# Conditioning weights from the SP queue to GpSimd's queue, with three buffers of their own

## The chip, the cores and the metric

The kernel runs on one core of a Trainium2 chip, as one program. The metric is the device time of one execution in microseconds. The kernel before took 1189.63, 1191.67 and 1193.36 us in three runs, median 1191.67. One more execution was recorded by the hardware profiler; the rows of the profile below are of that one.

## The reference, cut to what matters

Two layers of a decoder trunk work on 256 tokens of width 1024. Each layer has three sub-layers: a SwiGLU feed-forward, a token mixer (gated linear recurrence in layer 0, chunked gMLP in layer 1) and a second feed-forward. Every sub-layer is wrapped by two norms and by a shift, a scale and a gate, which come from one vector `c`:

```
cond = silu(c)
mod  = (cond @ ada_w[i] + ada_b[i]).reshape(9, 1024)      # 3 sub-layers x (shift, scale, gate)

def sublayer(x, fn, pre_g, post_g, shift, scale, gate, res_w):
    h = rms_norm(x, pre_g) * (1.0 + scale) + shift
    return x + res_w * gate * rms_norm(fn(h), post_g)
```

The matrix `ada_w` of the two layers has 2 x 1024 x 9216 float32 values. The kernel holds it as 144 tiles of 128 x 1024, that is 144 x 512 KB. These are the conditioning weights. The other weights are those of the feed-forwards and the mixers.

## The kernel before

**Stages.** The six sub-layers run one behind the other: ffn0, the recurrence (hg), ffn1, ffn2, the gMLP (gm) and ffn3. Each takes the normed activations (`h`, transposed, as a high and a low part), multiplies them with blocks of weights on TensorE, and ends in a tail (`tail`, L250): the last output products, the post norm, the new `x`, the next sub-layer's pre norm, and TensorE transposes to the new `h`.

**Weights.** A block of 1 MB comes in two halves (`wblock`, L112). Each half is loaded into one of four `raw` buffers on SP's queue (`load`, L55), ScalarE writes its rounded high part (L119), and VectorE writes the rest as the low part by a subtraction (L120). High and low part stand in tiles `w` of a pool of 12, enough for six blocks. Each product on TensorE is three matmuls: high x high, high x low, low x high. In ffn0 a 128 x 256 product takes three matmuls (`mm3f`, L332); later feed-forwards use `chunk2` (L322), 16 matmuls for a chunk; an output block (`out_mm`, L274) is 24 matmuls of 128 x 512.

**Conditioning.** For each of the 144 tiles, `ada` (L159) loads 512 KB and lets VectorE take the dot product with `cond` (L169: one instruction for the product and its sum, one that reads the sum out); the result is one column of `mod`. The text calls this pair a dot. The buffers are two tiles of the pool `adap`; in the start phase (`ring` is 1) two of three tiles come from the pool `p4` of four buffers instead. `pace` (L134) spreads the tiles over the blocks of weights: `wblock` counts a credit up and calls `ada` when it is due. Some 16 tiles have to be there before ffn0 can start, two for each 128 rows of the first product.

**The gate.** `gate_tile` (L188) turns eight columns of `mod` into the gate tile `G`, 128 x 1024. VectorE scales them (L193), TensorE transposes them (`gps`, L195), ScalarE copies the result (`grow`, L197), and two DMAs on GpSimd's queue write it to DRAM (`gflat`, L199) and read it back, spread to all partitions (`G`, L201). `G` is used in the tail by L259 and L263. Before the change these twelve DMAs are all that is on GpSimd's queue.

**The start.** `start` (L879) loads `c`, `x` in two halves and a few constants, computes `cond` through TensorE (`cps`, L897), the pre norm of `x` (L905 to L917) and transposes it (`xps`, L921). For each 128 rows, `first_h` (L938) then makes shift and `A` from two dots (L944, L945), ScalarE applies them (`hf`, L948) and writes the high part of `h` (L950), and VectorE writes the low part (L951). ffn0's first product (L418) is sorted so that in each of the first seven steps 16 matmuls of high x high stand first, then 16 with the low part of `h`, then 16 with the low part of `w`.

**What sets the order.** The program is written with a tile framework. Its scheduler orders the instructions of each engine by priorities and by a simulated time of its own; tile pools give the buffers, and an instruction that needs a buffer waits until the last reader of the old tile is done. `keep_in_program_order` holds the loads of one queue in the order in which the code issues them. Each engine and each queue takes its instructions strictly in the order that results.

Of the kernel before, what the change touches and what calls it, by code (L numbers as in the profile page):

```python
# [10 lines left out]
F32 = mybir.dt.float32  # L11
# [7 lines left out]
P = 128  # L19
# [14 lines left out]
class Body:  # L34
    def __init__(self, ctx, tc, ins, out):
        self.ctx, self.tc, self.nc, self.out = ctx, tc, tc.nc, out
        self.d = dict(zip(_INS, ins))
        pool = lambda name, bufs, **k: ctx.enter_context(tc.tile_pool(name=name, bufs=bufs, **k))
        self.const = pool("const", 1)
        self.raw = pool("raw", 4)  # L40
        self.whl = pool("whl", 12)
        self.act = pool("act", 1)
        self.adap = pool("adap", 2)
        self.cols = pool("cols", 2)
        self.tiny = pool("tiny", 4)
        self.bcp = pool("bcp", 2)
        self.p4 = pool("p4", 4)
        self.p2 = pool("p2", 4)
        self.scr = pool("scr", 1)
        self.acc = pool("acc", 4, space=PSUM)  # L50
        self.yps = pool("yps", 1, space=PSUM)
        self.dram = pool("dram", 2, space=bass.MemoryType.DRAM)
# [106 lines left out]
    def ada(self, upto):  # L159
        nc = self.nc  # L160
        while self.ada_next < min(upto, 144):
            i = self.ada_next
            if self.ring and i % 3:
                t = self.p4.tile([P, D], F32, tag="t4", name="ada")
            else:
                t = self.adap.tile([P, D], F32, tag="ada", name="ada")
            self.load(t, self.d["ada"][i])
            junk = self.scr.tile([P, D], BF16, tag="junkv", name="junkv")
            nc.vector.tensor_tensor_reduce(junk, t, self.cond, 1.0, 0.0, ALU.mult, ALU.add,  # L169
                                           self.mod[i // 24][:, i % 24:i % 24 + 1])  # L170
            self.ada_next += 1
# [313 lines left out]
    def hgrn(self, hT, G_fn, pre_next, nxt, bg):  # L485
        nc, tc = self.nc, self.tc
# [36 lines left out]

        def gate_f(hb, pr, z):

            L = self.adap.tile([P, 512], F32, tag="ada", name="L")
            c = slice(512 * pr, 512 * pr + 512)
            k, nk, b = kn[hb][:, c], kn[hb][:, H4:][:, c], bq[hb][:, c]
            nc.scalar.activation(L, z, AF.Abs)
            self.act_exp(L, L, scale=-1.0)  # L530
            self.tact(L, L, AF.Ln, bias=1.0)
            nc.vector.scalar_tensor_tensor(b, z, 0.0, L, op0=ALU.min, op1=ALU.subtract)
            nc.vector.scalar_tensor_tensor(nk, z, 0.0, L, op0=ALU.max, op1=ALU.add)
            hs = [(4 * hb + 2 * pr + i, slice(i * S, (i + 1) * S)) for i in range(2)]
            col = lambda a, h: a[:, h:h + 1]
            for h, sl in hs:
                nc.scalar.activation(L[:, sl], b[:, sl], AF.Abs, bias=col(self.ldiff, h))
            for h, sl in hs:
                nc.scalar.activation(b[:, sl], b[:, sl], AF.Relu, bias=col(self.ldiff, h))
            self.act_exp(L, L, scale=-1.0)  # L540
            self.tact(L, L, AF.Ln, bias=1.0)
            for h, sl in hs:
                nc.vector.scalar_tensor_tensor(b[:, sl], b[:, sl], col(self.loglb, h), L[:, sl],
                                               op0=ALU.add, op1=ALU.add)
                nc.vector.tensor_tensor_scan(b[:, sl], self.rmask, b[:, sl], 0.0, ALU.mult, ALU.add)
            for h, sl in hs:
                self.act_exp(k[:, sl], nk[:, sl], scale=-1.0, bias=col(self.log1mlb, h))
                nc.vector.scalar_tensor_tensor(nk[:, sl], nk[:, sl], col(self.log1mlb, h), b[:, sl],
                                               op0=ALU.subtract, op1=ALU.add)
# [172 lines left out]
        self.table("natural_log_exp_and_others")  # L722
        self.hg_cols()
        run(feat(lambda pr, ps: gate_f(0, pr, ps)))

        def q1_silu():
# [6 lines left out]
        zip_steps(attn(0, bank_y, ops[0]), [  # L733
            feat(lambda pr, ps: nc.scalar.copy(qs(1, pr), ps)), once(q1_silu),
            feat(lambda pr, ps: gate_f(1, pr, ps)),
            tok(lambda t, ps: nc.scalar.copy(v[:, t, 512:], ps))], 5)
        G = G_fn()
# [358 lines left out]
```

## Time and profile before

| | |
|---|---|
| median of three runs | 1191.67 us (1189.63 to 1193.36) |
| the profiled execution: its own time | 1193.24 us |
| the profiled execution: span, first to last instruction | 1191.5 us |
| mean granted TensorE clock | 0.984 |
| moved by the DMA engines | 282.32 MB, mean 237 GB/s |

In the rows of the profile, PE is TensorE's matmuls, PEld its weight loads, DVE VectorE, ACT ScalarE, POOL GpSimd, SP SyncE; an engine's name with a q behind it is its queue of DMAs or its sequencer. L169 is line 169 of the kernel. `out<-in` names the tiles that an instruction writes and reads. A row of the timeline has the start, the duration, the engine, the line, the operation, the tiles and how many instructions were merged, and in brackets the idle time before it with what ended it. A row of the waits has who waited for what, the total in us, how often, and the longest. A matmul's duration is modelled and overlaps with the next one, so the pace of TensorE is read from the distance of the starts.

### The profile page before, as it was taken

To read this page: it belongs to the slowest core of one execution; us is meant where nothing else is said; L and a number is where in the kernel's file an instruction comes from. 1 tells how busy PE (TensorE), PEld (TensorE's weight loads), DVE (VectorE), ACT (ScalarE), POOL (GpSimd) and SP (SyncE) were. 2 spreads that over 40 slices of the span, in tenths; PEclk is the share of its full clock that TensorE was granted. 3 is DMA by queue.
4 is the path that set the end of the run, shared out by engine and by line. 5 is a ranking of instruction groups with operands and counts; after the bars stand their busy time and mean duration, and the time that the engine had idled before them with its cause. 6 is when DMAs were issued, how large, how long until landed. Compare 5 with 4: busy or idle time off the path is not lost.

```text
span 1191.5 us, 17180 instructions
## 1 busy us (share of the span) xinstructions
PE 1146.5 (96%) x6518; PEld 995.4 (84%) x6518; DVE 888.8 (75%) x1331; ACT 657.2 (55%) x1054; POOL 6.8 (1%) x16
## 2 busy tenths in 40 slices
PE   7999999997997999999999999999999999999997
PEld 6999998797895788888778888888888887888886
DVE  6997888868887887787677787657978786666652
ACT  6464446648766754456655545554754457555541
POOL 0000000000000000000000000000000000000000
PEclk9999999997999999999999999999999999999999
DMA  9899998782335777887578888537777765666640
GB/s 345 311 314 318 333 327 314 251 285 101 124 95 185 263 267 272 278 272 262 173 251 267 282 269 272 188 124 261 277 254 262 248 212 177 203 222 233 213 137 36
DMA packets 79765, 282.32 MB, mean 237 GB/s; under 512 B 9873, under 2 KB 10561, under 8 KB 79682
## 3 DMA queue, kind: packets, MB, share of 16 engines
q1 hardware_dynamic: 78626, 278.05, 68.0%
q0 software_dynamic: 1056, 3.17, 0.8%
q8 instruction: 51, 0.84, 0.3%
q14 instruction: 32, 0.26, 0.1%
HBM read 280.11 MB, written 1.07 MB: 236 GB/s over the span
## 4 chain that ended last, share of the span: by engine, by line
PE 73%; DMA 10%; DVE 8%; ACT 5%; issue 3%; SPq 0%; DVEq 0%; ACTq 0%
PE ups L328 15%; PE ups L329 8%; PE y L144 7%; PE y L142 7%; PE y L143 7%; PE ups L418 4%; DMA ada<-in_ada 4%; DMA raw<-in_wffn 4%; DVE w L120 3%; PE ups L334 3%; PE ups L336 3%; PE ups L335 3%; DMA raw<-in_whg 3%; ACT w L119 2%; PE ab L599 2%
## 5 line engine op out<-in xcount | busy, mean ns | idle before, releaser
L120 DVE TENSOR_TENSOR w<-raw,w 128x1024 fp32r<-128x1024 f32 x376 | 453.5, 1220 | 84.7 <-ACT w L119 77.5
L119 ACT CAST w<-raw 128x1024 fp32r<-128x1024 f32 x376 | 388.0, 1050 | 202.9 <-DMA raw<-in_wffn 79.4
L328 PE MATMUL ups<-h,w 128*128 128x512 f32 x864 | 303.1, 394 | 0.0
L169 DVE CUSTOM_DVE_ANT_0 junkv<-ada,cond 128x1024 bf16<-128x1024 f32 x144 | 175.8, 1221 | 92.0 <-DMA ada<-in_ada 91.5
L329 PE MATMUL ups<-h,w 128*128 128x256 f32 x864 | 242.5, 281 | 0.0
L328 PEld LDWEIGHTS ups<-h,w 128*128 128x128 f32 x864 | 162.3, 188 | 36.8
L142 PE MATMUL y<-w,t 128*128 128x512 f32 x448 | 179.4, 400 | 4.5 <-ACT t L147 4.5
L143 PE MATMUL y<-w,t 128*128 128x512 f32 x448 | 178.2, 398 | 0.0
L144 PE MATMUL y<-w,t 128*128 128x512 f32 x448 | 177.6, 397 | 0.2
L329 PEld LDWEIGHTS ups<-h,w 128*128 128x128 f32 x864 | 163.7, 190 | 0.9
L334 PE MATMUL ups<-h,w 128*128 128x256 f32 x416 | 118.3, 285 | 0.6 <-ACT w L119 0.6
L336 PE MATMUL ups<-h,w 128*128 128x256 f32 x416 | 117.8, 283 | 0.2 <-DVE w L120 0.2
L335 PE MATMUL ups<-h,w 128*128 128x256 f32 x416 | 117.6, 283 | 0.0
L142 PEld LDWEIGHTS y<-w,t 128*128 128x128 f32 x448 | 84.5, 189 | 24.1 <-ACT t L147 5.3
L144 PEld LDWEIGHTS y<-w,t 128*128 128x128 f32 x448 | 84.3, 189 | 21.0 <-DVE t L148 1.1
L143 PEld LDWEIGHTS y<-w,t 128*128 128x128 f32 x448 | 84.5, 189 | 17.9
L79 ACT ACTIVATE t<-t 128x256 f32<-128x256 f32 (+2 forms) x70 | 36.3, 523 | 97.7 <-DVE t L378 95.5
L334 PEld LDWEIGHTS ups<-h,w 128*128 128x128 f32 x416 | 79.7, 192 | 1.7 <-ACT w L119 0.8
L335 PEld LDWEIGHTS ups<-h,w 128*128 128x128 f32 x416 | 79.7, 192 | 0.8 <-issue 0.2
L336 PEld LDWEIGHTS ups<-h,w 128*128 128x128 f32 x416 | 79.7, 192 | 0.4 <-DVE w L120 0.4
L291 PE MATMUL pps<-w,h 128*128 128x512 f32 x160 | 64.4, 403 | 5.3 <-DVE h L247 5.3
L292 PE MATMUL pps<-w,h 128*128 128x512 f32 x160 | 63.8, 399 | 0.0
(199 smaller groups left out, 1435.4 us busy)
## 6 DMA issues: line engine op xcount, KB each, us to landing
raw<-in_wffn SPq DMA_DIRECT2D x264, 512.0 KB, 5.5
ada<-in_ada SPq DMA_DIRECT2D x144, 512.0 KB, 6.5
raw<-in_wgmu SPq DMA_DIRECT2D x48, 512.0 KB, 5.2
raw<-in_whg SPq DMA_DIRECT2D x40, 512.0 KB, 5.8
raw<-in_wgmv SPq DMA_DIRECT2D x24, 512.0 KB, 5.0
G<-gflat POOLq DMA_DIRECT2D x6, 512.0 KB, 5.9
t<-in_gbin SPq DMA_DIRECT2D x6, 256.0 KB, 5.2
x<-in_x SPq DMA_DIRECT2D x2, 512.0 KB, 4.0
```

Source lines behind the costliest of these rows:

```text
L119: nc.scalar.copy(hi[:, sl], raw)
L120: nc.vector.tensor_sub(lo[:, sl], raw, hi[:, sl])
L142: self.paced(mm(ps, l[0], r[0], start=start, stop=False))
L143: mm(ps, l[0], r[1], start=False, stop=False)
L144: mm(ps, l[1], r[0], start=False, stop=stop)
L169: nc.vector.tensor_tensor_reduce(junk, t, self.cond, 1.0, 0.0, ALU.mult, ALU.add, self.mod[i // 24][:, i % 24:i % 24 + 1])
L291: mm(res[g][t], h(0, kc), u(0, kc), start=kc == 0, stop=False)
L328: self.paced(mm(ps, u[0], self.h2[:, :, :, kc, :], start=kc == 0, stop=False))
L329: mm(ps[:, 1, :], u[1], self.h2[:, 0, :, kc, :], start=False, stop=kc == KC - 1)
L334: self.paced(mm(o, u[0], h[0], start=start, stop=False))
L335: mm(o, u[0], h[1], start=False, stop=False)
L336: mm(o, u[1], h[0], start=False, stop=stop)
```

## The change

The load of a conditioning tile moves from SP's queue to GpSimd's, again in program order. The pool `adap` gets three buffers instead of two. The tile `L` of the recurrence's gate (`gate_f`, L524), which shared the buffers of `adap`, gets its own: a new pool `lp` with one buffer for one half, and the scratch tile `hf` for the other half. Each line behind L44 moves down by one.

```diff
-        self.adap = pool("adap", 2)
+        self.adap = pool("adap", 3)
+        self.lp = pool("lp", 1)
...
-            self.load(t, self.d["ada"][i])
+            self.tc.keep_in_program_order(nc.gpsimd.dma_start(t, self.d["ada"][i]))
...
-            L = self.adap.tile([P, 512], F32, tag="ada", name="L")
+            L = self.lp.tile([P, 512], F32, tag="L", name="L") if pr else self.scr.tile([P, 512], F32, tag="hf", name="L")
```

The scheduler then orders anew. Three places matter below.

SP's queue in ffn0, before the change. `raw` is half a block of weights, `ada` a conditioning tile, the five tiles from `npost` on are constants:

```order
L56 DMA raw<-in_wffn 128x1024 x4
L56 DMA npost<-in_npost 128x48
L56 DMA lb<-in_lb 128x24
L56 DMA lmask<-in_lmask 128x448
L56 DMA rmask<-in_rmask 128x256
L56 DMA onorm<-in_onorm 128x1
L56 DMA raw<-in_wffn 128x1024 x2
L56 DMA ada<-in_ada 128x1024
```

GpSimd's queue after it, from its first DMA on; the gates' `gflat` and `G` stand between runs of conditioning tiles:

```order
L168 DMA ada<-in_ada 128x1024 x33
L200 DMA gflat<-grow 8x128
L202 DMA G<-gflat 128x1024
L168 DMA ada<-in_ada 128x1024 x31
L200 DMA gflat<-grow 8x128
L202 DMA G<-gflat 128x1024
L168 DMA ada<-in_ada 128x1024 x21
L200 DMA gflat<-grow 8x128
```

SP's queue now holds the weights, `x`, the constants and the output alone. The conditioning tiles stand on GpSimd's queue, and the 34th tile, for one, stands behind the `gflat` and the `G` of ffn0.

VectorE in the start phase, before (L905 is the sum of squares of one half of `x`, L907 to L915 the pre norm, `mod` the result of a dot):

```order
L905 ISA yg,s_125<-x_100 128x1024
L905 ISA s_125 128x1
L928 TENSOR_SCALAR ab_167<-adab 128x8
L907 TENSOR_SCALAR v<-s_125 128x2
L909 RECIPROCAL r<-v 128x2
L915 TENSOR_SCALAR xn<-x_99,r 128x512
L915 TENSOR_SCALAR yg<-x_100,r 128x512
L169 ISA junkv,mod_103<-ada,cond 128x1024
L169 ISA mod_103 128x1
L944 TENSOR_TENSOR shift<-mod_103,adab 128x1
```

and after, from the second dot on (the first stands between the two sums of squares):

```order
L170 ISA junkv,mod_106<-ada,cond 128x1024
L170 ISA mod_106 128x1
L908 TENSOR_SCALAR v<-s_128 128x2
L945 TENSOR_TENSOR shift<-mod_106,adab 128x1
L946 SCALAR_TENSOR_TENSOR A<-mod_106,ab_170,npre 128x1
L170 ISA junkv,mod_106<-ada,cond 128x1024
L170 ISA mod_106 128x1
L910 RECIPROCAL r<-v 128x2
L170 ISA junkv,mod_106<-ada,cond 128x1024
L170 ISA mod_106 128x1
L916 TENSOR_SCALAR xn<-x_102,r 128x512
L916 TENSOR_SCALAR yg<-x_103,r 128x512
```

Before, no dot stands ahead of `xn` and `yg`; now four do. Eight dots stand ahead of the first low part of `h` (L951), where there were two.

VectorE at the end of ffn0, around the last but one unit (`t_1862` before and `t_1865` after are the same tile, the product of that unit; `shift` is that of the next sub-layer), before:

```order
L169 ISA junkv,mod_104<-ada,cond 128x1024
L169 ISA mod_104 128x1
L120 TENSOR_TENSOR w<-raw,w 128x1024 x2
L169 ISA junkv,mod_104<-ada,cond 128x1024
L169 ISA mod_104 128x1
L182 TENSOR_TENSOR shift<-mod_104,adab 128x8
L367 TENSOR_TENSOR t_1862<-t_1862,ups 128x512
L120 TENSOR_TENSOR w<-raw,w 128x1024
L148 TENSOR_TENSOR t_1863<-t_1862,t_1863 128x512
```

and after:

```order
L368 TENSOR_TENSOR t_1680<-t_1680,ups 128x512
L121 TENSOR_TENSOR w<-raw,w 128x1024
L149 TENSOR_TENSOR t_1681<-t_1680,t_1681 128x512
L121 TENSOR_TENSOR w<-raw,w 128x1024 x5
L170 ISA junkv,mod_107<-ada,cond 128x1024
L170 ISA mod_107 128x1
L170 ISA junkv,mod_107<-ada,cond 128x1024
L170 ISA mod_107 128x1
L368 TENSOR_TENSOR t_1865<-t_1865,ups 128x512
L170 ISA junkv,mod_107<-ada,cond 128x1024
L170 ISA mod_107 128x1
L121 TENSOR_TENSOR w<-raw,w 128x1024
```

Before, a dot stood behind every two or so subtractions. Now the three units ahead of the first dot shown, which is the 34th, have none at all. From there to the tail they stand close, 14 dots from this row to the tail's first VectorE instruction (`be`, L218).

## Prediction

> **What bounds the kernel now.** I read the page first, then windows and the timeline, the waits last. All durations are of the profiled execution (its own time 1193.24 us, 1.7 us of it outside the span).
>
> ```profile
> span 1191.5 us, 17180 instructions
> 58.00:190.00 132.00, 132.00 (x918) 122.91 (x917) 109.55 (x144) 68.14 (x78) 1.21 (x2) 1.00 0.92 328
> 420.00:570.00 150.00, 150.00 (x787) 127.89 (x786) 111.73 (x160) 76.37 (x121) 1.08 (x2) 1.00 0.79 269
> 615.00:765.00 150.00, 150.00 (x790) 127.95 (x789) 110.84 (x155) 76.06 (x119) 1.07 (x2) 1.00 0.79 266
> 120.12 0.39 PE L144 MATMUL y<-w,t 128*128 128x512 f32 x1
> 120.35 0.40 PE L142 MATMUL y<-w,t 128*128 128x512 f32 x1
> 121.05 0.28 PE L334 MATMUL ups<-h,w 128*128 128x256 f32 x1
> 121.17 0.27 PE L335 MATMUL ups<-h,w 128*128 128x256 f32 x1
> ```
>
> In the three feed-forward windows (columns: length; busy time and count of PE, PEld, DVE, ACT, POOL; clock; DMA share; GB/s) TensorE has no idle time, and VectorE is busy 109.55 of 132 and about 111 of 150 us. The starts show the pace: 0.23 us for a matmul of 512 columns, 0.12 us for one of 256. Here nothing that helps a queue can gain; time is lost or won only where TensorE waits: the start, the tails, the recurrence and the gMLP.
>
> ```profile
> DVE junkv L169 <- DMA ada<-in_ada: 91.5, 51, 5.4
> SPq L56 <- DVE mod L169: 77.2, 42, 6.2
> PE fps L336 <- DVE w L120: 3.1, 2, 1.7
> PE ots L663 <- DVE t L658: 4.4, 1, 4.4
> PE y L142 <- ACT t L147: 2.4, 1, 2.4
> PE vps L854 <- DVE t L861: 1.6, 2, 1.2
> PE y L142 <- ACT t L147: 1.3, 1, 1.3
> ```
>
> VectorE waits 91.5 us for conditioning tiles, and SP's queue 77.2 us for a dot to free a buffer, with weights queued behind. But the waits of TensorE that VectorE's or ScalarE's work on weights and products ends, and that a freer SP queue could shorten, are only 3.1 + 4.4 + 2.4 + 1.6 + 1.3 = 12.8 us (the five PE rows, from windows 265 to 300, 360 to 420, 570 to 615 and 840 to 1025 us).
>
> **The change part by part.** *SP's queue loses 144 loads and the 77.2 us of waits:* a gain between 0 and 12.8 us. The raw loads still wait for their four buffers, which the subtractions free. I take half, 6 us.
>
> *The start.* Rows of its chain:
>
> ```profile
> 0.00:16.00 16.00, 7.43 (x21) 4.44 (x21) 6.79 (x17) 10.51 (x16) 0.20 (x4) 1.00 0.87 317
> 1.15 0.82 SPq L56 DMA_DIRECT2D x<-in_x  x2
> 9.37 0.49 DVE L915 TENSOR_SCALAR xn<-x,r 128x512 f32<-128x512 f32 x1
> 10.16 1.22 DVE L169 CUSTOM_DVE_ANT_0 junkv<-ada,cond 128x1024 bf16<-128x1024 f32 x1
> 11.31 0.08 DVE L169 DVE_READ_ACCUMULATOR2_ANT mod<- 128x1 f32 x1
> 15.99 44.22 PE L418 MATMUL ups<-h,w 128*128 128x256 f32 x350 [2.41 <-ACT h L950]
> 16.81 0.42 DVE L951 TENSOR_TENSOR h<-hf,h 128x256 fp32r<-128x256 f32 x1
> ```
>
> A dot is 1.22 + 0.08 = 1.30 us. Four dots now stand ahead of `xn`: 5.2 us on the chain `xn`, transposes, copies, `hf`, first product at 15.99. Less some 0.2 us that the square root covers, the lower bound is 5. The upper bound is the low part of `h`, behind eight dots: if both queues are served evenly, eight conditioning tiles, two halves of `x` and four raw halves have landed by then, 14 x 0.524 MB = 7.3 MB, at 317 GB/s 23 us from 1.2, so 24.3; one dot and L951 end it at 26.0. TensorE wanted it after 16 matmuls of 0.12 us, at 17.9: 8 us late. From here on 16.00 to 58 us TensorE has no idle time to give it back. I take 7, nearer to the upper bound, as `x` itself now shares the engines with tiles issued from the first microsecond.
>
> [...]
>
> *The gates.* GpSimd's queue holds its order, so a conditioning tile behind a gate waits for `grow`, for `gflat` to land and for `G` to be issued. VectorE waits in its own order for the dot, with subtractions, products and the tail queued behind, and TensorE waits for those. Gates of ffn0 and ffn1:
>
> ```profile
> 155.25 0.28 PE L195 MATMUL gps<-ident,gate 128*8 128x128 f32 x1
> 156.12 0.65 POOL L199 DMA_DIRECT2D gflat<-grow  x1 [155.67 <-ACT grow L197]
> 162.88 0.56 POOL L201 DMA_DIRECT2D G<-gflat  x1 [6.11 <-DMA gflat<-grow]
> 526.67 0.28 PE L195 MATMUL gps<-ident,gate 128*8 128x128 f32 x1
> 532.87 0.52 POOL L199 DMA_DIRECT2D gflat<-grow  x1 [218.75 <-ACT grow L197]
> 536.42 0.55 POOL L201 DMA_DIRECT2D G<-gflat  x1 [3.03 <-DVE w L120]
> ada<-in_ada SPq DMA_DIRECT2D x144, 512.0 KB, 6.5
> G<-gflat POOLq DMA_DIRECT2D x6, 512.0 KB, 5.9
> L120 DVE TENSOR_TENSOR w<-raw,w 128x1024 fp32r<-128x1024 f32 x376 | 453.5, 1220 | 84.7 <-ACT w L119 77.5 <-issue 4.5 <-PE y L143 0.9
> L148 DVE TENSOR_TENSOR t<-t,t 128x512 fp32r<-128x512 f32 x50 | 34.1, 685 | 3.5 <-ACT t L147 3.4
> L378 DVE TENSOR_TENSOR t<-t,ups 128x256 f32<-128x256 f32 x54 | 22.4, 415 | 3.1 <-ACT t L377 3.0
> 194.69 0.15 DVE L218 TENSOR_SCALAR be<-s 128x1 f32<-128x1 f32 x1 [1.38 <-ACT junka L216]
> 155.00:195.00 40.00, 32.15 (x43) 1.00 0.93 332
> 155.00:195.00 40.00, 11.04 (x18) 1.00 0.93 332
> ```
>
> ffn0, from `gps` at 0: `G` is issued at 162.88 - 155.25 = 7.6, the 34th tile 0.6 later, and it lands 6.5 after that, at 14.7. VectorE has reached that dot by 9.8: two casts, two subtractions and the freeing of a weight tile after one unit of 48 x 0.12 = 5.8. It waits 4.9 us. Up to the last product part (L148) then stand 11 dots, 7 subtractions and 4 instructions of 0.69: 14.3 + 8.5 + 2.8 + 0.5 for three small ones = 26.1, done at 40.8. TensorE's work up to there is four units and two output blocks and 12 matmuls: 4 x 5.8 + 2 x 24 x 0.23 + 2.8 = 36.9, and it stalls 3.9. Then `be` stands behind three dots and three subtractions, 40.8 + 7.6 = 48.4, where its input is there at 36.9 + 3.9 + 1.4 + 0.6 = 42.8: the tail starts 5.6 late. Before, VectorE had 9 dots (18 instructions, 11.04 us) in this stretch and was busy 32.15 of 40 us, which left room for this; 14 dots and the wait don't fit. Sum 9.5, taken 9. Lower bound 2: the tile lands by 9.8, and the tail, which has fewer subtractions, makes some up. Upper bound 17: dots are then paced by three buffers, (1.3 + 0.6 + 6.5) / 3 = 2.8 us each, 3.4 more on the stall and 4 on the tail.
>
> ffn1: `G` was issued 9.8 after `gps`, of that 6.2 for `grow`; with `grow` at once as in ffn0, 4.5. The first dot can start between 11.6 and 16.9; I take 13. Behind it stand 8 dots, 10 subtractions, 6 of 0.42, 4 of 0.69: 10.4 + 12.2 + 2.5 + 2.8 + 0.5 = 28.4, done at 41.4. TensorE needs it after eight chunks of 8 x 0.35 = 2.8, two output blocks and 12 matmuls, 36.2: stall 5.2. The tail comes 3 late by the same count: 8, between 2 and 14. ffn2: 8 dots, 9 subtractions, 26.7 us, done at 39.7, stall 3.5, no dots in the tail: 4, between 0 and 9. Gates of the recurrence and the gMLP: VectorE gets there about when the tile does: 1, between 0 and 4. Behind ffn3's gate no tile is left.
>
> *The third buffer, and `L` in buffers of its own:* nothing; the cover is that `L`'s new places are free by the time of the recurrence, and without it a wait of one dot, 1.3 us.
>
> Sum: 7 + 9 + 8 + 4 + 1 - 6 = +23 on 1193.24, that is 1216.2; the profiled execution stands 1.6 over the median of the runs shown, so 1215.
>
> **The rivals.** *A freer queue wins.* If tiles that are issued early land well ahead, no dot waits, the gates cost nothing, all 12.8 us of TensorE's waits close and the start costs only its lower 5: 1191.7 - 7.8 = 1184. For it: 91.5 us of dots that wait now. Against it: those waits lie beside a busy TensorE. It decides where the 34th tile has landed before VectorE gets to it, under 9.8 us behind `gps`. Chance 0.12.
>
> *The gates are hidden, the start is not:* 7 + 1 - 6 = +2, 1194, between 1184 and 1201. For it: the scheduler placed the dots by its own times, and VectorE has 8 us of room in 40. Chance 0.2.
>
> *The forecast:* start and gates cost: 1201 (gain nothing, 5 + 2 + 2) to 1232 (upper bounds less 12.8). Chance 0.6.
>
> *All upper bounds, no gain:* 8 + 17 + 14 + 9 + 4 = +52, 1244: dots paced by the landing of three buffers wherever they stand close. Chance 0.08.
>
> **How the numbers follow.** About 0.3%, 3.6 us, is what a measurement can tell from no change: 1188.1 to 1195.3. The first rival is faster, 0.12. The second lies half in that band: same 0.1. Slower is 0.1 + 0.6 + 0.08 = 0.78. Range 1190 to 1238: it leaves out the first rival and most of the last.
>
> **What would show it.** Right: the first L418 at 21 to 24 us; the first dot behind each gate waiting for its tile; idle TensorE in the tails of ffn0 and ffn1 of 5 to 10 us more each. SP's waits for a dot gone, and VectorE's waits for tiles bunched behind the gates. Wrong: the first L418 by 17 us, or no long wait of L170 behind `G`, or a tail of ffn0 that ends as soon after `gps` as before.

## The result and the profile after

The changed kernel takes 1256.36 us (median of four runs, 1252.50 to 1257.93), the kernel before in the same comparison 1191.17. The ratio is 1.0541, 95% interval 1.0511 to 1.0571: slower by some 65 us. The forecast of 1215 had the sign; the size is outside its range, which ended at 1238. The profiled execution took 1255.85 us, its span is 62.6 longer than that of before.

The first rows of the page and of the waits after (who waited for what: total, times, longest, in us):

```profile
span 1254.1 us, 17255 instructions
...
POOL gflat L200 <- ACT grow L198: 655.2, 6, 214.2
POOL ada L168 <- DVE mod L170: 316.6, 80, 14.7
...
DVE junkv L170 <- DMA ada<-in_ada: 59.4, 33, 6.3
```

The waits of SP's queue, before and after:

```profile
SPq L56 <- DVE w L120: 588.0, 246, 19.1
SPq L56 <- DVE t L378: 143.9, 41, 7.5
SPq L56 <- DVE mod L169: 77.2, 42, 6.2
```

```profile
SPq L57 <- DVE w L121: 809.1, 296, 26.6
SPq L57 <- DVE t L379: 150.1, 25, 7.8
```

SP's wait for a dot is gone, as forecast, and VectorE waits less for tiles (59.4 us, before 91.5). But SP's wait for VectorE's subtractions has grown by 221.1 us: the weights wait for the same engine at another instruction (the second row, for a product, is nearly the same in both). And GpSimd's queue stands for 655.2 us, half of the program, before the `gflat` of the next gate. In that time none of the tiles behind it is issued; they go through in the other half.

Where the time went is read from the starts of TensorE's matmuls in the timeline. The table has the time from one landmark to the next, in us: the first product of ffn0; `gps` of ffn0; the first transpose (`npa`) of each of the first five tails; in the recurrence the first L600 (L599 before).

| from, to | before | after | difference |
|---|---|---|---|
| start, first product | 16.0 | 21.6 | +5.6 |
| first product, `gps` of ffn0 | 139.3 | 147.4 | +8.1 |
| `gps`, tail of ffn0 | 49.5 | 62.7 | +13.2 |
| tail of ffn0, first L600 | 81.4 | 73.8 | -7.6 |
| first L600, tail of the recurrence | 97.5 | 105.0 | +7.5 |
| to the tail of ffn1 | 193.2 | 207.0 | +13.8 |
| to the tail of ffn2 | 193.8 | 198.6 | +4.8 |
| to the tail of the gMLP | 220.8 | 238.3 | +17.5 |
| to the last matmul | 193.4 | 193.1 | -0.3 |

**The start.** The timeline after, to be held against the rows of xn, the first L418 and L951:

```profile
11.12 0.17 DVE L929 TENSOR_SCALAR ab<-adab 128x8 f32<-128x8 f32 x1 [1.36 <-DMA adab<-in_adab]
...
15.09 0.48 DVE L916 TENSOR_SCALAR xn<-x,r 128x512 f32<-128x512 f32 x1
...
21.56 2.72 PE L419 MATMUL ups<-h,w 128*128 128x256 f32 x11 [2.90 <-ACT h L951]
...
23.34 0.42 DVE L952 TENSOR_TENSOR h<-hf,h 128x256 fp32r<-128x256 f32 x1
```

`xn` is 5.7 us late and the first product 5.6, in size as worked out. Part of that is luck: in the timeline the four dots take 4.6 us from start to next start, and 1.36 us is a wait for the small tile `adab` to land, which the forecast didn't have. At 70 us stands a second loss that the forecast didn't have. First the timeline, then windows of 2 us (length; busy time and count of PE, PEld, DVE, ACT, POOL; clock; DMA share; GB/s):

```profile
73.57 1.04 ACT L120 CAST w<-raw 128x1024 fp32r<-128x1024 f32 x1 [2.23 <-DMA raw<-in_wffn]
74.53 0.59 ACT L80 ACTIVATE t<-ups 128x512 f32<-128x512 f32 x1
75.17 0.58 PE L335 MATMUL ups<-h,w 128*128 128x256 f32 x1 [5.14 <-ACT t L80]
```

```profile
72.00:74.00 2.00, 0.00 (x0) 0.00 (x0) 1.02 (x1) 0.43 (x1) 0.53 (x1) 1.00 1.05 420
74.00:76.00 2.00, 0.83 (x4) 0.83 (x5) 1.35 (x2) 2.00 (x4) 0.00 (x0) 0.56 0.97 334
76.00:78.00 2.00, 2.00 (x11) 2.00 (x11) 2.00 (x4) 2.00 (x5) 0.09 (x1) 0.50 1.02 395
78.00:80.00 2.00, 2.00 (x11) 2.00 (x11) 2.00 (x4) 1.47 (x3) 0.44 (x1) 0.50 0.93 277
80.00:82.00 2.00, 2.00 (x15) 2.00 (x14) 1.84 (x4) 1.68 (x4) 0.00 (x0) 0.73 0.75 250
82.00:84.00 2.00, 2.00 (x19) 2.00 (x18) 2.00 (x3) 1.57 (x2) 0.00 (x0) 1.00 0.58 221
```

ScalarE's cast waits for weights, and behind it stands the activation (L80) that reads the accumulator which TensorE needs next. TensorE idles for 5.1 us, and then its granted clock is 0.50: 11 matmuls in 2 us in place of 19.

**The gate of ffn0 and its tail.** The timeline after:

```profile
168.96 0.28 PE L196 MATMUL gps<-ident,gate 128*8 128x128 f32 x1
172.64 0.53 POOL L202 DMA_DIRECT2D G<-gflat  x1 [1.71 <-DMA gflat<-grow]
180.75 1.23 DVE L170 CUSTOM_DVE_ANT_0 junkv<-ada,cond 128x1024 bf16<-128x1024 f32 x1 [2.07 <-DMA ada<-in_ada]
...
225.08 1.23 DVE L170 CUSTOM_DVE_ANT_0 junkv<-ada,cond 128x1024 bf16<-128x1024 f32 x1 [2.79 <-DMA ada<-in_ada]
226.23 0.08 DVE L170 DVE_READ_ACCUMULATOR2_ANT mod<- 128x1 f32 x1
226.23 0.16 DVE L225 RECIPROCAL r<-sq 128x1 f32<-128x1 f32 x1
226.31 0.67 DVE L264 TENSOR_TENSOR yg<-y,G 128x512 f32<-128x512 f32 x1
```

The first dot behind the gate starts 11.8 us after `gps`, earlier than the 14.7 worked out (`G` waits 1.71 us for `gflat` to land, before 6.11). The later row matters as much: dots stand within the tail's own chain, between `be` and `r`, and one waits 2.79 us for its tile there. The count of the forecast stopped at `be`.

**The clumps.** Windows of VectorE's dots alone (length; busy time and number of instructions, two for a dot; clock; DMA share; GB/s), around the gate of ffn0, before and after:

```profile
118.00:170.00 52.00, 14.73 (x24) 1.00 0.93 337
170.00:205.00 35.00, 11.04 (x18) 1.00 0.89 309
```

```profile
118.00:170.00 52.00, 3.68 (x6) 1.00 0.68 230
170.00:232.00 62.00, 23.38 (x38) 0.94 0.86 303
```

Three dots in 52 us where there were twelve, then 19 in 62. In the gMLP, from `vps` on, before and after:

```profile
856.00:944.00 88.00, 12.99 (x21) 1.00 0.75 257
944.00:991.00 47.00, 5.45 (x10) 1.00 0.71 235
```

```profile
902.00:990.00 88.00, 26.13 (x43) 0.92 0.84 285
990.00:1054.00 64.00, 0.91 (x2) 1.00 0.56 188
```

Behind the fifth gate no other gate holds a tile: twice as many dots stand in the first 88 us, and after 991 us there are none to the end of the program, where before they went on to 1110. TensorE waits among them, by 7.5 us at the longest, for a tile that ScalarE scales (L853). The factors for it come from VectorE (`rr`, L101), where they stand behind two of the dots, the first of which waits 2.1 us for its tile:

```profile
909.92 0.80 PE L855 MATMUL vps<-w 128*128 128x128 f32 x2 [7.54 <-ACT w L853]
```

The order shows the same for the whole program. Dots per 12 subtractions of weights, in VectorE's order, from ffn0 to ffn3 (the last 16 subtractions have none in any of them):

| kernel | dots per 12 subtractions |
|---|---|
| before, e1, e7, e8 | 12, 6, 7, 7, 7, 8, 12, 5, 0, 3, 6, 7, 6, 6, 1, 4, 7, 6, 6, 2, 0, 3, 4, 4, 4, 5, 0, 2, 1, 3 |
| after | 12, 8, 7, 6, 0, 14, 17, 0, 6, 12, 3, 0, 0, 6, 9, 7, 5, 0, 0, 7, 2, 0, 5, 10, 8, 0, 0, 0, 0, 0 |
| e3 | 12, 8, 7, 15, 28, 5, 20, 9, 6, 11, 9, 10, 4, 0, and none from there |
| e5 | 12, 6, 7, 7, 1, 14, 12, 5, 0, 2, 6, 7, 6, 6, 1, 5, 6, 6, 3, 6, 0, 3, 4, 4, 4, 5, 0, 1, 2, 3 |

On SP's queue each tile stood between two loads of weights, and the weights paced the dots. On GpSimd's queue a tile comes when a buffer is free and no gate stands ahead (its two waits above, 316.6 and 655.2 us), and the scheduler put the dots there.

### The profile page after: what moved, and what is told of

Same layout as the page of the kernel before. It is cut to its first block, busy times and chain, and to the rows that moved or that the text cites. A ratio compares the mean times of both kernels' runs of the same rounds, so it can differ in the third digit from the quotient of the medians.

```text
span 1254.1 us, 17255 instructions
## 1 busy us (share of the span) xinstructions
PE 1163.6 (93%) x6518; PEld 1004.2 (80%) x6518; DVE 885.7 (71%) x1331; ACT 662.0 (53%) x1054; POOL 82.6 (7%) x160
## 5 line engine op out<-in xcount | busy, mean ns | idle before, releaser
L170 DVE CUSTOM_DVE_ANT_0 junkv<-ada,cond 128x1024 bf16<-128x1024 f32 x144 | 175.7, 1220 | 60.2 <-DMA ada<-in_ada 59.4
L143 PE MATMUL y<-w,t 128*128 128x512 f32 x448 | 183.6, 410 | 15.6 <-ACT t L148 15.6
L145 PE MATMUL y<-w,t 128*128 128x512 f32 x448 | 182.4, 408 | 3.7 <-DVE t L149 3.6
L144 PE MATMUL y<-w,t 128*128 128x512 f32 x448 | 181.5, 405 | 0.0
L143 PEld LDWEIGHTS y<-w,t 128*128 128x128 f32 x448 | 87.0, 194 | 36.9 <-ACT t L148 17.6
L145 PEld LDWEIGHTS y<-w,t 128*128 128x128 f32 x448 | 87.1, 194 | 26.6 <-DVE t L149 6.1
L168 POOL DMA_DIRECT2D ada<-in_ada x144 | 76.1, 530 | 449.1 <-DVE mod L170 316.6
L144 PEld LDWEIGHTS y<-w,t 128*128 128x128 f32 x448 | 87.0, 194 | 18.9
L336 PEld LDWEIGHTS ups<-h,w 128*128 128x128 f32 x416 | 81.4, 196 | 0.8 <-issue 0.2
L337 PEld LDWEIGHTS ups<-h,w 128*128 128x128 f32 x416 | 81.4, 196 | 0.4 <-DVE w L121 0.4
```

Of the source, the lines that this page charges most:

```text
L143: self.paced(mm(ps, l[0], r[0], start=start, stop=False))
L144: mm(ps, l[0], r[1], start=False, stop=False)
L145: mm(ps, l[1], r[0], start=False, stop=stop)
L336: mm(o, u[0], h[1], start=False, stop=False)
L337: mm(o, u[1], h[0], start=False, stop=stop)
```

## The experiments

Two theories went in. "Gates" is the one of the forecast: a tile behind a gate waits, VectorE waits in its order, the rest is late. "Clumps" says that the dots, freed from the weights, stand close in VectorE's order and delay its other work, gate or no gate. Times are medians; ratios are to the kernel before on the same chip, with 95% intervals. 0.01 of a ratio is 11.9 us.

**e1, buffers alone.** The changed kernel with the load on SP's queue again.

```diff
-            self.tc.keep_in_program_order(nc.gpsimd.dma_start(t, self.d["ada"][i]))
+            self.load(t, self.d["ada"][i])
```

> The three buffers and the separate L alone; the conditioning tiles stay on SP's queue. VectorE's order of dots is then that of before (per 12 subtractions 12, 6, 7, 7, 7, 8, 12, 5 dots). Theory 'gates' (a tile behind a gate on GpSimd's queue waits for it, VectorE waits in its order, the rest is late by that) and theory 'clumps' (freed from the queue of weights, the dots are no longer spread over the blocks of weights but stand in clumps in VectorE's order, which make its work on products and weights late, gate or no gate) both expect the time of before, 1188 to 1194 us. A rival, that the buffers or L's new places cost something, expects over 1196 us.

1183.91 us, ratio 0.9931 (0.9901 to 0.9961): 0.7% faster, and the interval leaves out 1. Both theories and the rival were wrong about it. The gain lies between the tail of ffn0 and the first L600, 70.7 us in place of 81.4. So the loss by the queue is larger than 65 us.

**e2, GpSimd's queue doesn't wait for a gate's values.**

```diff
-        nc.gpsimd.dma_start(flat, row)
+        nc.scalar.dma_start(flat, row)
...
-        nc.gpsimd.dma_start(G, flat.rearrange("k p -> (k p)").unsqueeze(0).to_broadcast([P, D]))
+        nc.gpsimd.dma_start(G, self.d["ada"][s])
```

> As the changed kernel, but nothing on GpSimd's queue waits for a gate: gflat is written on ScalarE's queue, and G on GpSimd's queue reads a tile of conditioning weights instead of gflat (the gates' values are left out of the result, which is wrong for that; all instructions and the bytes of G stay). The dots still stand in clumps, now up to 15 per 12 subtractions in ffn0. Theory 'gates': the losses at the ends of ffn0, ffn1, ffn2 (together some 35 us) go, 1210 to 1225 us, with no wait of VectorE for a tile behind a gate. Theory 'clumps': they stay or move, 1235 to 1265 us.

1249.83 us, ratio 1.0500 (1.0471 to 1.0528). That is the number of "clumps", but the run decides less than it was meant to. Its waits:

```profile
POOL G L202 <- DVE yg L264: 588.1, 5, 172.2
POOL ada L168 <- DVE mod L170: 277.3, 87, 11.1
```

`G` now stands on the queue until the tail before has freed its buffer, 588.1 us in all. The queue was held nearly as long as in the changed kernel, only by another wait.

**e3, gates on SP's queue.**

```diff
-        nc.gpsimd.dma_start(flat, row)
+        nc.sync.dma_start(flat, row)
...
-        nc.gpsimd.dma_start(G, flat.rearrange("k p -> (k p)").unsqueeze(0).to_broadcast([P, D]))
+        nc.sync.dma_start(G, flat.rearrange("k p -> (k p)").unsqueeze(0).to_broadcast([P, D]))
```

> As the changed kernel, but gflat and G go on SP's queue; GpSimd's queue holds the 144 conditioning tiles alone. The dots run still further ahead in VectorE's order (28 in one stretch of 12 subtractions, all done by the middle of the program). SP's weights now wait for the gates. Theory 'gates': the wait moves to the weights, which have four buffers ahead; 1205 to 1235 us. Theory 'clumps': 1240 to 1275 us, with TensorE losing its time early, where the clumps are, and no loss after the middle of ffn2.

1318.70 us, ratio 1.1057 (1.1015 to 1.1100). With GpSimd's queue free of gates it is the slowest but e4; both ranges are missed on the high side. Two costs stand in it. The dots (a window of dots alone) from `gps` to the tail of ffn0, 101 us long where before had 49.5, and SP's wait for `grow`:

```profile
170.00:271.00 101.00, 36.92 (x60) 0.79 0.86 308
```

```profile
SPq L200 <- ACT grow L198: 174.8, 5, 45.2
```

30 dots take 36.92 us of VectorE there, and the weights stop for up to 45.2 us. The forecast for "clumps" that nothing is lost after the middle of ffn2 was wrong too: its tail takes 60.0 us where before took 47.3. e10 separates the two costs.

**e4, subtractions and dots held in the code's order.**

```diff
-            nc.vector.tensor_sub(lo[:, sl], raw, hi[:, sl])
+            self.tc.keep_in_program_order(nc.vector.tensor_sub(lo[:, sl], raw, hi[:, sl]))
...
-            nc.vector.tensor_tensor_reduce(junk, t, self.cond, 1.0, 0.0, ALU.mult, ALU.add,
-                                           self.mod[i // 24][:, i % 24:i % 24 + 1])
+            self.tc.keep_in_program_order(nc.vector.tensor_tensor_reduce(junk, t, self.cond, 1.0, 0.0, ALU.mult, ALU.add,
+                                           self.mod[i // 24][:, i % 24:i % 24 + 1]))
```

> As the changed kernel (GpSimd's queue, three buffers, gates on the same queue), but VectorE's subtractions of weights and the dots hold the order in which the code issues them, so that the dots are spread over the weights as before (12, 6, 7, 7, 7, 8, 12, 5 per 12 subtractions). Theory 'clumps': most of the loss goes, 1195 to 1215 us; what is left is the start (0 to 6 us) and one wait behind each gate. Theory 'gates': a tile wanted in the code's order still stands behind a gate on the queue, and the waits get no shorter, 1240 to 1265 us.

1427.30 us, ratio 1.1982 (1.1957 to 1.2006). Neither theory had that. The edit did more than spread the dots: the scheduler put the held subtractions behind products that come late. The timeline in the gMLP shows VectorE idle for 8 us with weights to be split behind it:

```profile
1043.24 0.48 DVE L862 SCALAR_TENSOR_TENSOR t<-vps,glng,bc 128x256 f32<-128x256 f32 x1 [7.96 <-PE vps L855]
```

So e4 says nothing on clumps. The next run has the narrower edit.

**e5, no dot ahead of its weights.** An order between two instructions of VectorE, and nothing else held:

```diff
-            nc.vector.tensor_sub(lo[:, sl], raw, hi[:, sl])
+            self.sub = nc.vector.tensor_sub(lo[:, sl], raw, hi[:, sl])
...
-            nc.vector.tensor_tensor_reduce(junk, t, self.cond, 1.0, 0.0, ALU.mult, ALU.add,
+            dot = nc.vector.tensor_tensor_reduce(junk, t, self.cond, 1.0, 0.0, ALU.mult, ALU.add,
                                            self.mod[i // 24][:, i % 24:i % 24 + 1])
+            if not self.ring:
+                self.after(dot, self.sub)
```

> As the changed kernel (GpSimd's queue, gates on it, three buffers), with one edit: a dot may not stand ahead of the last subtraction that the code issued before it. Nothing else is held, so VectorE's order has the dots spread as before (per 12 subtractions 12, 6, 7, 7, 1, 14, 12, 5, 0, 2, 6, 7), but for a hole and a clump at the gate of ffn0 and a small one at that of ffn2. Theory 'clumps': the losses of the ends of ffn1 (12 us), of the recurrence (8 to 9) and of the gMLP (17) go; the start (13 with the stall at 70 us) and ffn0's end (14) stay: 1256 - 38 = 1218 us, 1208 to 1228. Theory 'queue' (GpSimd's queue itself costs, by its DMAs or by sharing the engines with SP's): at least 1240 us.

1226.89 us, ratio 1.0276 (1.0243 to 1.0308): inside the range of "clumps". The rule takes back 0.0265, 31.6 us. The places are in part others than expected. By the starts in the two traces, 12.5 us come back between the tails of the recurrence and of ffn1, as expected, but 9.6 instead of 17 up to the tail of the gMLP, about nothing in the recurrence, and 6.7 at the end of ffn0, which was to stay. So the total in the range is in part luck. From the first `vps` to its tail the gMLP takes 141.6 us (after 152.7, before 135.2); its dots in the first 88 us are as many as before the change:

```profile
897.00:985.00 88.00, 12.26 (x20) 1.00 0.75 242
```

**e6, and the first 16 tiles on SP's queue.**

```diff
-            self.tc.keep_in_program_order(nc.gpsimd.dma_start(t, self.d["ada"][i]))
+            if i < 16:
+                self.load(t, self.d["ada"][i])
+            else:
+                self.tc.keep_in_program_order(nc.gpsimd.dma_start(t, self.d["ada"][i]))
```

> As e5, and the first 16 tiles (those of the start phase) on SP's queue as before the change. Theory 'start' (tiles issued from the first microsecond take the DMA engines from x and the first weights, and more dots stand ahead): the first product of ffn0 at 16 us again instead of 21, no stall of TensorE at 70 us, 10 to 13 us less than e5. If the stall at 70 us has another cause, only 5 us less than e5.

1211.97 us, ratio 1.0154 (1.0121 to 1.0188), 14.5 us less than e5, a little more than expected. The first product and the window that held the stall (PE is the first busy time):

```profile
15.89 6.32 PE L424 MATMUL ups<-h,w 128*128 128x256 f32 x28 [2.41 <-ACT h L956]
```

```profile
58.00:80.00 22.00, 22.00 (x170) 21.28 (x169) 19.90 (x26) 14.47 (x20) 1.59 (x3) 1.00 0.80 274
```

Both losses are gone, so the stall at 70 us belongs to the start.

**e7 and e8, L alone and the third buffer alone,** both on SP's queue.

```diff
+        self.lp = pool("lp", 1)
...
-            L = self.adap.tile([P, 512], F32, tag="ada", name="L")
+            L = self.lp.tile([P, 512], F32, tag="L", name="L") if pr else self.scr.tile([P, 512], F32, tag="hf", name="L")
```

> The kernel before with L in buffers of its own, two buffers for conditioning tiles as before, on SP's queue. With e8 it splits the gain of e1 (7.7 us of the median, 10 of them in the first half of the recurrence). If L held up SP's queue there (L stands in a buffer of the tiles, so that tiles and the weights behind them wait for it): 1182 to 1187 us. If the third buffer gives the gain: 1189 to 1193 us.

```diff
-        self.adap = pool("adap", 2)
+        self.adap = pool("adap", 3)
```

> The kernel before with three buffers for conditioning tiles, which L still shares, on SP's queue. If L held up SP's queue in the recurrence, a third buffer helps too, but less: 1186 to 1191 us. If the gain of e1 is the third buffer's: 1182 to 1186 us.

e7: 1192.21 us, ratio 0.9991 (0.9971 to 1.0010). e8: 1183.28 us, ratio 0.9905 (0.9877 to 0.9934). The gain is the third buffer's. The waits of SP's queue for a dot, in e7 and in e8:

```profile
SPq L57 <- DVE mod L170: 73.7, 42, 6.1
```

```profile
SPq L56 <- DVE mod L169: 32.7, 23, 5.1
```

**e9, and no wait for a gate's values.** The edits of e2 on e6.

> As e6 (GpSimd's queue, dots not ahead of their block of weights, first 16 tiles on SP's queue), and GpSimd's queue waits for no gate: gflat is written on ScalarE's queue, and G reads a tile of conditioning weights (the gates' values are left out of the result). VectorE's order then has the dots spread as before throughout (12, 6, 7, 7, 7, 8, 12, 5, 0, 2, 6, 7 per 12 subtractions). If what is left of the loss in e6 (28 us over e1) is the gates' hold on the queue: 1183 to 1192 us, the ends of ffn0, ffn1 and ffn2 in about 49.5, 50 and 47 us. If it is GpSimd's queue itself or the two queues' sharing: 1203 us or more.

1189.28 us, ratio 0.9981 (0.9963 to 1.0000), 20.6 us less than e6 and inside the range of "gates". From `gps` to the first transpose of the tail, e6 and e9: ffn0 58.6 and 47.9, ffn1 54.9 and 47.3, ffn2 52.3 and 47.3. The rest of the program gives some 4 us back. By the order, e9 also spreads the dots that stand close behind the gates of ffn0 and ffn2 in e6, so the difference is the wait and these dots together.

**e10, gates on SP's queue.** The edits of e3 on e6.

> As e6, with gflat and G on SP's queue; nothing is left out. GpSimd's queue then holds conditioning tiles alone, and the weights on SP's queue wait for each gate some 8 us with four buffers ahead of them. If the weights' buffers cover that: 1183 to 1195 us, a version of the change without its loss. If not: 1200 to 1230 us, with ScalarE waiting for weights behind each gate.

1263.32 us, ratio 1.0592 (1.0553 to 1.0630): worse than either range. SP's queue holds its order too:

```profile
SPq L205 <- ACT grow L203: 185.8, 6, 38.1
```

The weights stop for up to 38.1 us, more than four buffers cover. Beside e3, where SP's wait is nearly the same (174.8 us), it is 0.0465 or 55 us shorter. If the start is 14.5 of that, as between e5 and e6, clumps with no gate on their queue cost some 41 us there; this is an estimate, as no run has that step alone.

**e11, the control.** The rule of e5 on e1, SP's queue.

> The control of e5's edit: the kernel of e1 (SP's queue, three buffers, L apart) with the rule that a dot may not stand ahead of the last subtraction issued before it. On SP's queue the dots hardly move. Theory 'clumps' expects the time of e1, 1180 to 1188 us; if the rule costs or gains something by itself, this shows it, and e5, e6, e9 and e10 are read against it.

1181.53 us, ratio 0.9910 (0.9877 to 0.9942). The rule by itself is worth nothing that can be measured beside e1. e11 and e8 are the fastest here, both faster than before and after; no run tells the two apart.

**e12, the queue alone,** with two buffers and L as before.

> The kernel before with the loads on GpSimd's queue, two buffers, L in a buffer of the tiles as before. VectorE's order has clumps of 11, 17, 10, 12 dots per 12 subtractions where the changed kernel has 14, 17, 12, 9. If the third buffer takes part of the landing off the dots behind a gate, and 9 us in the recurrence as in e8: 1262 to 1280 us. If clumps are all: 1250 to 1262 us.

1269.37 us, ratio 1.0649 (1.0604 to 1.0694), inside the range in which the third buffer helps. The queue by itself costs 77 us, and the third buffer (with `L`) gives 13 of it back.

**e13, one G.** As e9, and `G` is loaded once.

```diff
-        G = self.act.tile([P, D], F32, tag="G", name="G")
-        nc.gpsimd.dma_start(G, self.d["ada"][s])
-        return G
+        if s == 0:
+            self.G0 = self.act.tile([P, D], F32, tag="G", name="G")
+            nc.gpsimd.dma_start(self.G0, self.d["ada"][s])
+        return self.G0
```

> As e9, but G is loaded once, at the start, and used in all six tails (the gates' values are left out of the result, and five loads of 512 KB). In e9 the queue was still held: the trace shows G waiting there for the buffer that the tail before frees, 239 us in five waits, with conditioning tiles behind it. Here nothing but conditioning tiles stands on GpSimd's queue. If that hold is the 7.8 us by which e9 is longer than its twin on SP's queue (e11, 1181.5): 1178 to 1184 us. If it is GpSimd's queue itself, or two queues sharing the engines: 1186 to 1190 us.

1185.19 us, ratio 0.9946 (0.9916 to 0.9976), between the two ranges. In e9 `G` had still waited on the queue for its buffer:

```profile
POOL G L207 <- DVE yg L269: 239.0, 5, 126.4
```

Without that 0.0035 goes, and to e11 another 0.0036, some 4 us, is left; in both steps the intervals overlap. The small sum hides larger parts of both signs: in the traces (one of each) e13 takes 11.7 us longer than e11 from the tail of ffn0 to that of the recurrence and 5.2 longer from the tail of ffn2 to that of the gMLP, and is shorter elsewhere. A slower landing isn't it: the median from issue to landing of a tile is 6.1 us on GpSimd's queue in e13 and 6.9 on SP's in e11. Whether GpSimd's queue costs anything by itself stays open.

## Why the prediction was wrong, point by point

The table goes from before by e11, e9, e6 and e5 to the changed kernel. Each part is a difference of ratios times 1191 us, so the parts add up by construction, and they hold for this order of the steps. In another order they are others: e2 takes the gates' values off the queue of the changed kernel itself and gives 4.9 us back, not 20.6, because `G` then holds the queue in their place.

| part | runs | measured | forecast |
|---|---|---|---|
| third buffer (with L) | e11 to before | -10.7 | 0 |
| queue itself, hold by `G`'s buffer | e9 less e11 | +8.5 | -6 |
| gates | e6 less e9 | +20.6 | +22 |
| start | e5 less e6 | +14.5 | +7 |
| clumps | after less e5 | +31.6 | not in the sum |
| sum (ratio 1.0541) | | +64.4 | +23 |

**The gates** were right, in mechanism and, on this path, in size: forecast 9, 8, 4 and 1 for ffn0, ffn1, ffn2 and the others; e6 less e9 gives 10.8, 7.7 and 5.0 in the three tails and no net loss elsewhere. The signs that the prediction named for being right came as well: the first product at 21.6 us, and first dots that wait 2.1, 6.4, 4.9 and 2.1 us behind the gates of ffn0, ffn1, ffn2 and the gMLP. Signs that are taken at the start and the gates alone don't show whether a cost elsewhere is missing. Details were off in both directions, the tile's landing (11.8 us behind `gps`, not 14.7) and the dots behind `be`.

**The start** was right as far as it was followed: 5.6 us at the first product, between the bounds of 5 and 8. What failed is the end of the account: it asked only whether TensorE could give the delay back up to 58 us, and put the weights, which were late as well, at nothing. At 70 us TensorE paid 5.1 us for them and then ran at a granted clock of 0.50; the start measured 14.5 us in place of 7.

**The freed SP queue** gave no gain in total. The 12.8 us of TensorE's waits that were to gain from it were in part real (7.6 us went in the recurrence), but e8 closes them on SP's queue with a third buffer, and e9, with the queue free of its worst, is no faster than e11. In e9 VectorE waits for tiles for 5.0 us in all (before 91.5), so these waits were beside a busy TensorE, as the prediction says against its first rival. The wait of 77.2 us for dots had been read as the price of sharing a queue; more than half of it was the price of two buffers (32.7 us in e8).

**The third buffer** was costed at nothing, its cover being `L`'s places. It is worth 11.3 us alone (e8), the largest single error on the good side.

**The clumps** are the step that broke the forecast: the sum has no term for dots that stand close, except behind a gate. The order of ffn0 was on the table, no dot in three units and then 14; the sum priced it only behind the gates of ffn0, ffn1 and ffn2, and gave the recurrence and the gMLP 1 us, because VectorE gets to the gate's tile about when it lands there. That is nearly true (a wait of 2.1 us in the gMLP) and beside the point: the dots behind it then run as close as buffers allow. Held back in e5, they give 31.6 us back. The stretch up to the tail of the gMLP lost 17.5 us, of which e5 takes back 9.6; some 5 stay with tiles on GpSimd's queue even where the dots are spread and no gate holds it (226.8 us in e13, 221.5 in e11), and no run shows why. What had to be counted is the number of dots in each stretch of VectorE's order, through the whole program, and not only at the gates. None of the rivals had this mechanism: the one with all upper bounds has dots that stand close, but in the same places, and ended at 1244. (The upper end of the forecast's own sum, 1232, should read 1231: 39.2 on 1191.7.)

## What to carry to other kernels

In this kernel the loads that shared an in-order queue with the main stream were paced by that stream. Taken off it, their consumers were placed where buffers and other waits of the new queue allowed. So count the moved instructions per stretch of the busy engine's order over the whole program before pricing any single wait. When a change bundles a queue with a buffer, time the buffer alone: here it was the gain, and the queue the loss.

## What was not expected of the hardware

Some stalls of TensorE cost more than their length here. The trace records the granted clock in pieces. Behind such a stall it is 0.50 for 3.4, 6.8 or 10.2 us; behind the one at 70 us, from 74.2 to 81.1 us, as in the windows from 74 to 82 us above. Up to the last matmul, before has 7 such pieces, 34.1 us together, and after 13 with 68.2 (its record begins at 26.4 us). What that costs can be counted over the timeline: matmuls of 512 and 256 columns whose distance to the next start is between 1.5 and 2.3 times the 0.23 or 0.12 us that the starts show elsewhere, four or more in a row, the excess summed. Before loses 7.2 us in 6 such stretches, after 17.1 in 10. So by this estimate about 10 of the 62.6 us are clock, on top of the stalls themselves; no term of the forecast had it. The length of a stall alone doesn't tell which: in the trace of before the clock goes to 0.50 at 611.1 us behind a stall of 2.4 us (606.9 to 609.3), and in that of after it stays at 1.00 behind one of 3.0 us that ends at 444.1.
